# A SwiGLU channel mixer: twelve column pairs as seven half-size products, with the weight sums made by adding DMA transfers

## The chip, the cores and the metric

The kernel runs on one core of one Trainium2 chip. The metric is the device time of one execution in microseconds (us). The core has five engines with a queue each: TensorE (PE; its weight loads are listed apart as PEld), VectorE (DVE), ScalarE (ACT), GpSimd (POOL) and SyncE (SP, which only starts DMA transfers). Sixteen DMA engines move the data; transfers started by SP and ACT go through hardware queues, those started by POOL through a software queue.

## The reference

One encoder block on x of 512 frames by 1024 channels, in float32. Two token mixers (a gated delta rule and a convolution) are merged and added to x; the channel mixer follows:

```python
x = x + (gate_a * out_a + gate_b * out_b) @ w_out[l]

h2 = rmsnorm(x, norm2_w[l])
f_gate, f_up = jnp.split(h2 @ ffn_w_gate_up[l], 2, axis=-1)
x = x + (jax.nn.silu(f_gate) * f_up) @ ffn_w_down[l]
...
return rmsnorm(x, norm_f_w)
```

The hidden width is 2816, that is 22 tiles of 128. `h2 @ ffn_w_gate_up` is the part that the change recasts; `ffn_w_down` is read by both versions in the same seven products.

## The kernel before

Every float32 factor of a large product is split into a high part (type float32r) and a low part. One product of tiles is three matmuls: high by high, high by low, low by high (`split3`, line 107; all matmuls of the large products carry line 113).

**Weights.** `unit` (line 92) brings in 512 KB of weights: SP loads tile `raw` (128x1024), ACT makes the high part `whi` (line 102), DVE the low part `wlo` (line 104). The pool `wp` holds three of each, so a unit's split can begin when PE has finished with the unit three places back.

**Order.** A list scheduler lays out each engine's queue. It takes instructions by priority, which is program order unless an offset is given (`background`, line 618), as soon as operands and buffers are free in its own simulated time. `issue_after` pins one instruction behind another on the same engine. Each engine then executes its queue strictly in order.

**Stages.** The projections of the token mixers run to about 497 us; their last ones are the 16 gate projections, a unit each (line 555), each with a 256 KB store. Then come 8 units of `wo` and 8 of `wpw` (lines 734 to 760), then `tok_mm` with `w_out`, 4 units for each half of the channels (line 763). Its `post`, `norm2`, makes the RMS norm of the rows, whose transposes become `hh` and `hl`, the high and low part of h2 (8 channel tiles of 128x512).

**Gate and up** (line 873). For each of the 22 hidden tiles f two units are used: `wgu[f]` (gate) and `wgu[22 + f]` (up). `col_tile` makes 8 channel tiles x 3 = 24 matmuls of 512 columns for each, so a pair is 48. ACT applies SiLU, DVE multiplies (line 888). The first pair is cut in two halves of 256 columns (`k_loop`). Beside this loop POOL makes the weight sums of the down projection: `sums(k)` (line 860) loads 1 MB of `wdn`, adds four times 128x512 (lines 864 to 867) and writes 1 MB to DRAM. DVE and ACT make the operands of the down projection from the hidden tiles: for f < 11 the split of the first half of the tokens, for f >= 11 sums of two hidden tiles.

**Down** (lines 933 to 1016). Four rounds: `two` runs three times over 11 weight pairs with four 128x512 accumulators (12 matmuls of 512 columns for each weight pair), then the last product, p3. Its six units `ws` are loaded and split (line 994) while `part` consumes them: k = 0 to 5 for both row tiles, k = 6 to 10 for row tile 0, then row tile 1 in two halves of 256 columns. Between the third `two` and p3 the program has `norm_f` of the row tiles (lines 983 to 988): ACT squares (line 794), POOL sums and the power (lines 796, 798), POOL's product of the rows with the norm weight (line 916), ACT's scaling (line 918) and DVE's (line 920), then the stores. The residual y1 stays in SBUF from `tok_mm` to the end.

Of the kernel before, what the change touches and what calls it, by code (L numbers as in the profile page):

```python
# [6 lines left out]
F32 = mybir.dt.float32  # L7
# [23 lines left out]
def block_kernel(ctx, tc, a):  # L31
# [6 lines left out]
    pa_ = ctx.enter_context(tc.tile_pool(name="pA", bufs=1))  # L38
# [53 lines left out]
    def unit(ap):  # L92
        n = 1024
        raw = wp.tile([P, 1024], F32, name="raw")
        if isinstance(ap, tuple):
            n = T * len(ap)
            for i, p in enumerate(ap):
                nc.sync.dma_start(raw[:, i * T:(i + 1) * T], p)
        else:
            nc.sync.dma_start(raw.rearrange("p (a c) -> p a c", a=2) if len(ap.shape) == 3 else raw, ap)  # L100
        hi = wp.tile([P, 1024], F32R, name="whi")
        marked(S.activation(hi[:, 0:n], raw[:, 0:n], AF.Copy), "unit")  # L102
        lo = wp.tile([P, 1024], F32R, name="wlo")
        marked(V.tensor_tensor(out=lo[:, 0:n], in0=raw[:, 0:n], in1=hi[:, 0:n].bitcast(F32), op=ALU.subtract), "unit")  # L104
        return hi, lo
# [28 lines left out]
    cs = []  # L134

# [426 lines left out]
    def ln_mean():  # L562
# [5 lines left out]
        for i in range(KD):  # L568
            V.tensor_tensor(out=cv[i], in0=cv[i], in1=mu, op=ALU.subtract)
            if i == 0:  # L570
                S.activation(vacc, cv[i], AF.Square)
            else:
                sq2 = tp.tile([P, T], F32, name="acc4")
                S.activation(sq2, cv[i], AF.Square)
                G.tensor_tensor(out=vacc, in0=vacc, in1=sq2, op=ALU.add)
# [111 lines left out]
    last = [None]  # L687
# [74 lines left out]

    def tok_mm(wname, kts, xh, xl, post, between):


        for hf in range(2):
# [25 lines left out]
    def rms_half(ss, hf, n, cs, sq, last):  # L792
# [47 lines left out]
    keep.close()  # L840


    fp = ctx.enter_context(tc.tile_pool(name="fp", bufs=2))
    nfw = fp.tile([P, D], F32, name="nfw", bufs=1)
    nc.gpsimd.dma_start(nfw, a["nfw"].partition_broadcast(P))
    FK = FF // 2

    def xset():

        return fp.tile([P, T], F32R, name="fh", bufs=FK + 2), fp.tile([P, T], F32R, name="fl", bufs=FK + 2)  # L850

# [3 lines left out]


# [3 lines left out]
    def sums(k):  # L860
        r = fp.tile([P, 4, T], F32, name="wst", bufs=1)
        nc.gpsimd.dma_start(r, a["wdn"][k].rearrange("p (i c) -> p i c", i=4))
        b11, b12, b21, b22 = (r[:, i, :] for i in range(4))
        G.tensor_tensor(out=b11, in0=b12, in1=b11, op=ALU.subtract)  # L864
        G.tensor_tensor(out=b12, in0=b22, in1=b12, op=ALU.subtract)
        G.tensor_tensor(out=b22, in0=b22, in1=b11, op=ALU.subtract)
        G.tensor_tensor(out=b21, in0=b22, in1=b21, op=ALU.subtract)
        nc.gpsimd.dma_start(wsum[k], r)

    TH = T // 2  # L870
    t1, t2 = slice(0, TH), slice(TH, T)
    fms, set1 = [], []
    for f in range(FF):
# [6 lines left out]
        sg = fp.tile([P, T], F32, name="fsg")  # L880
# [5 lines left out]
        fm = fp.tile([P, T], F32, name="fm", bufs=FF)  # L886
        fms.append(fm)
        V.tensor_tensor(out=fm, in0=pu, in1=sg, op=ALU.mult)  # L888
        if f < FK:
            sums(f)  # L890
            set1.append(xset())
            hi, lo = (t[:, t1] for t in set1[f])
            xsplit(hi, lo, fm[:, t1])
        else:

            b = fms[f - FK]
            s1 = fp.tile([P, TH], F32, name="s1")
            V.tensor_tensor(out=s1, in0=b[:, t2], in1=fm[:, t2], op=ALU.add)
            hi, lo = (t[:, t2] for t in set1[f - FK])
            xsplit(hi, lo, s1)  # L900
            V.tensor_tensor(out=b[:, t2], in0=b[:, t1], in1=b[:, t2], op=ALU.subtract)
            V.tensor_tensor(out=b[:, t1], in0=s1, in1=b[:, t1], op=ALU.subtract)


    hps.close()
    dp = ctx.enter_context(tc.tile_pool(name="dp", bufs=2, side="right"))
    ss3 = dp.tile([P, 5, NT], F32, name="ss3", bufs=1)
    o0 = [dp.tile([P, T], F32, name="o0", bufs=NT) for _ in range(NT)]
    c1, c2 = slice(0, T), slice(T, D)

    def norm_f(hf, n, cs):
        last = hf == 4 or hf == 1 and n != 1
        rms_half(ss3, hf, n, cs, dp.tile([P, T], F32, name="rms_sq", bufs=1)[:, 0:cs.stop - cs.start], last)
        rs = ss3[:, 3, n:n + 1]
        if hf == 0:
            G.tensor_tensor(out=o0[n], in0=y1[:, n, cs], in1=nfw[:, cs], op=ALU.mult)
        if last:
            S.activation(o0[n], o0[n], AF.Copy, scale=rs)
            o1 = dp.tile([P, T], F32, name="o1")
            V.scalar_tensor_tensor(out=o1, in0=y1[:, n, c2], scalar=rs, in1=nfw[:, c2], op0=ALU.mult, op1=ALU.mult)  # L920
# [154 lines left out]
```

## Time and profile before

| | |
|---|---|
| runs shown | 988.28, 990.41, 992.32 us; median 990.41 |
| the profiled execution | 987.57 us, its span 985.8 us |
| mean granted TensorE clock | 0.994 |
| PE busy | 955.7 us of the span (97%) |
| DVE, ACT, POOL busy | 669.8, 513.6, 255.1 us |
| moved by DMA | 138.50 MB, mean 140 GB/s |

A row of a timeline has start, duration, engine, line, operation, output <- inputs, and in brackets how long the engine had been idle and what ended that. A row of groups has the line, engine, operation and shapes, the count, then busy us and the mean ns of one, then the idle time before them. A row of a chain of waits has start, duration, engine, output and line. A row of windows has the stretch, its length, then the busy time (and instruction count) of PE, PEld, DVE, ACT and POOL, the granted clock, the share of the 16 DMA engines, and GB/s. A matmul's duration runs from its start to its modelled end; matmuls overlap, so the pace is read from start to start.

### The profile page before, as it was taken

To read this page: it belongs to the slowest core of one execution; us is meant where nothing else is said; L and a number is where in the kernel's file an instruction comes from. 1 tells how busy PE (TensorE), PEld (TensorE's weight loads), DVE (VectorE), ACT (ScalarE), POOL (GpSimd) and SP (SyncE) were. 2 spreads that over 40 slices of the span, in tenths; PEclk is the share of its full clock that TensorE was granted. 3 is DMA by queue.
4 is the path that set the end of the run, shared out by engine and by line. 5 is a ranking of instruction groups with operands and counts; after the bars stand their busy time and mean duration, and the time that the engine had idled before them with its cause. 6 is when DMAs were issued, how large, how long until landed. Compare 5 with 4: busy or idle time off the path is not lost.

```text
span 985.8 us, 13439 instructions
## 1 busy us (share of the span) xinstructions
PE 955.7 (97%) x4775; PEld 785.7 (80%) x4775; DVE 669.8 (68%) x1044; ACT 513.6 (52%) x1062; POOL 255.1 (26%) x410
## 2 busy tenths in 40 slices
PE   7999999999999999999999999999999999999995
PEld 5688878878787778888878888888888888888784
DVE  4899888888787669889578544542434464469953
ACT  6689777777767664543446323432223322256543
POOL 0314543343243240000050001243534432001412
PEclk9999999999999999999999999999999999999997
DMA  8233421413212122234744432556565565256462
GB/s 317 88 119 120 120 91 41 127 68 98 77 65 88 65 87 69 97 124 144 272 137 137 146 115 65 166 192 246 186 242 206 203 211 184 92 168 196 160 207 86
DMA packets 48291, 138.50 MB, mean 140 GB/s; under 512 B 7472, under 2 KB 9424, under 8 KB 45408
## 3 DMA queue, kind: packets, MB, share of 16 engines
q1 hardware_dynamic: 44016, 112.36, 34.4%
q0 software_dynamic: 3488, 24.17, 6.9%
q10 hardware_dynamic: 720, 1.11, 0.3%
q8 instruction: 37, 0.61, 0.3%
q14 instruction: 30, 0.25, 0.1%
HBM read 119.52 MB, written 18.10 MB: 140 GB/s over the span
## 4 chain that ended last, share of the span: by engine, by line
PE 84%; ACT 5%; DVE 4%; POOL 4%; issue 2%; DMA 1%; SPq 0%; POOLq 0%; ACTq 0%; DVEq 0%
PE mm L113 64%; PE w L113 11%; DVE wlo L104 1%; POOL Un L350 1%; ACT cp L355 1%; ACT Un L349 1%; PE st L477 1%; PE b L415 1%; PE b L421 1%; PE st L483 1%; POOL ytm L376 1%; PE st L489 1%; PE g L346 1%; DMA raw<-in_win_dram 1%; PE st L478 1%
## 5 line engine op out<-in xcount | busy, mean ns | idle before, releaser
L102 ACT ACTIVATE whi<-raw 128x1024 fp32r<-128x1024 f32 x167 | 176.1, 1057 | 327.1 <-PE mm L113 191.9
L113 PE MATMUL mm<-hh,whi 128*128 128x512 f32 x816 | 325.9, 400 | 0.0
L113 PE MATMUL mm<-hl,whi 128*128 128x512 f32 x816 | 321.9, 395 | 2.3 <-POOL hl L229 1.6
L113 PE MATMUL mm<-hh,wlo 128*128 128x512 f32 x816 | 322.3, 395 | 0.0
L104 DVE TENSOR_TENSOR wlo<-raw,whi 128x1024 fp32r<-128x1024 f32 x167 | 214.5, 1285 | 114.7 <-ACT whi L102 114.1
L545 DVE SCALAR_TENSOR_TENSOR cps<-c,c31w,cps 128x512 f32<-128x512 f32 x240 | 180.0, 750 | 4.9 <-ACT cps L543 1.0
L113 PEld LDWEIGHTS mm<-hl,whi 128*128 128x128 f32 x816 | 153.5, 188 | 33.0 <-POOL hl L229 2.9
L113 PEld LDWEIGHTS mm<-hh,wlo 128*128 128x128 f32 x816 | 153.4, 188 | 30.1
L113 PEld LDWEIGHTS mm<-hh,whi 128*128 128x128 f32 x816 | 153.5, 188 | 29.2 <-ACT hh L228 0.2
L888 DVE TENSOR_TENSOR fm<-mm,fsg 128x512 f32<-128x512 f32 x21 | 14.5, 692 | 67.0 <-PE mm L113 67.0
L300 DVE SCALAR_TENSOR_TENSOR acc<-mm,c4w,acc 128x509 f32<-128x509 f32 (+2 forms) x72 | 52.6, 738 | 1.5 <-ACT acc L297 1.2
L376 POOL TENSOR_TENSOR ytm<-U,y 128x60 f32<-128x60 f32 (+14 forms) x120 | 36.9, 307 | 60.6 <-DMA U<-sc 51.9
L113 PE MATMUL mm<-yh,whi 128*128 128x512 f32 x128 | 50.6, 396 | 0.0
L113 PE MATMUL mm<-yh,wlo 128*128 128x512 f32 x128 | 49.8, 389 | 0.0
L113 PE MATMUL mm<-yl,whi 128*128 128x512 f32 x128 | 49.8, 389 | 0.0
L113 PE MATMUL w<-whi,fh 128*128 128x512 f32 (+1 forms) x115 | 45.3, 395 | 2.8 <-ACT whi L102 2.8
L113 PE MATMUL w<-wlo,fh 128*128 128x512 f32 (+1 forms) x115 | 45.6, 397 | 2.4 <-DVE wlo L104 2.4
L113 PE MATMUL w<-whi,fl 128*128 128x512 f32 (+1 forms) x115 | 45.0, 393 | 0.0
L378 POOL TENSOR_TENSOR y<-y,ytm 128x60 f32<-128x60 f32 (+14 forms) x120 | 34.9, 291 | 9.4
L511 POOL TENSOR_TENSOR ss<-ss,half 128x4 f32<-128x4 f32 x8 | 8.1, 1014 | 109.5 <-DVE ss L509 109.5
L796 POOL TENSOR_SCALAR ss<-ss 128x1 f32<-128x1 f32 x17 | 5.7, 338 | 117.9 <-ACT sg L794 105.3
L864 POOL TENSOR_TENSOR wst<-wst 128x512 f32<-128x512 f32 x11 | 15.2, 1386 | 62.7 <-DMA wst<-in_wdn_dram 62.7
(288 smaller groups left out, 1489.1 us busy)
## 6 DMA issues: line engine op xcount, KB each, us to landing
raw<-in_win_dram SPq DMA_DIRECT2D x61, 512.0 KB, 3.3
raw<-in_wgu_dram SPq DMA_DIRECT2D x44, 512.0 KB, 3.4
wst<-in_wdn_dram POOLq DMA_DIRECT2D x11, 1024.0 KB, 5.7
wsum<-wst POOLq DMA_DIRECT2D x11, 1024.0 KB, 4.7
raw<-wsum SPq DMA_DIRECT2D x44, 256.0 KB, 3.2
raw<-in_wdn_dram SPq DMA_DIRECT2D x33, 256.0 KB, 2.9
A<-in_x_dram SPq DMA_DIRECT2D x8, 512.0 KB, 6.3
U<-sc SPq DMA_DIRECT2D x64, 64.0 KB, 2.3
```

Of the source, the lines that this page charges most:

```text
L102: marked(S.activation(hi[:, 0:n], raw[:, 0:n], AF.Copy), "unit")
L104: marked(V.tensor_tensor(out=lo[:, 0:n], in0=raw[:, 0:n], in1=hi[:, 0:n].bitcast(F32), op=ALU.subtract), "unit")
L113: marked(PE.matmul(ps, l, r, start=first and i == 0, stop=last and i == 2))
L300: marked(V.scalar_tensor_tensor(out=acc[:, s:], in0=ps[:, :T - s], scalar=c4w[:, j, k:k + 1], in1=acc[:, s:], op0=ALU.mult, op1=ALU.add))
L346: PE.matmul(ps[:, n, :], kT[:, n, :], kT[:, n, :], start=True, stop=True)
L349: S.activation(Un[:, n, :], ps[:, n, :], AF.Copy, scale=nb2[:, n:n + 1])
L350: G.tensor_tensor(out=Un, in0=Un, in1=DT, op=ALU.mult)
L376: G.tensor_tensor(out=tm[:, :, 0:w], in0=U[:, k, :, k + 1:], in1=y[:, :, k:k + 1].broadcast_to([P, NT, w]), op=ALU.mult)
L378: last[0] = G.tensor_tensor(out=y[:, :, k + 1:], in0=y[:, :, k + 1:], in1=tm[:, :, 0:w], op=ALU.add)
L545: V.scalar_tensor_tensor(out=acc, in0=c[:, k:k + T], scalar=c31w[:, i, k:k + 1], in1=acc, op0=ALU.mult, op1=ALU.add)
L864: G.tensor_tensor(out=b11, in0=b12, in1=b11, op=ALU.subtract)
L888: V.tensor_tensor(out=fm, in0=pu, in1=sg, op=ALU.mult)
```

## The change

For f = 0 to 9 gate and up stay as they were. For f = 10 to 21 the pair is treated as a 2x2 block matrix (gate and up, by two halves of the channels) times another (two halves of the channels by two halves of the tokens), and made by seven products (Strassen's scheme in Winograd's form) in place of eight: each is 4 channel tiles x 3 = 12 matmuls of 256 columns, 84 for a pair. The operand sums of h2 (`xb`, T1 to T4) are made once on DVE, POOL and ACT. The four sums of weights for each pair (s1 to s4, 256 KB each) are made in DRAM: SP copies one block, then a POOL transfer adds the other to it. These 48 pairs of transfers are issued one with each `unit`, from step 335 of the first stage on. A pair now takes four units (3.5 x 512 KB).

The weight sums of the down projection (`dsums`, as `sums` before) are spread over f = 1 to 16; five of the eleven lie beside the pairs 10, 11, 13, 14 and 16. The splits of hidden tiles 0 to 9 are made beside the pairs 10 to 14, two for each. Of the sums of hidden tiles two go to POOL. The residual is written to DRAM in `norm2` (`ysp`) and loaded again in the first `two` (`y2`). In `two` the next operands are made two steps later. The norm of the row tiles is spread over the first steps of p3; row tiles 2 and 3 are scaled by DVE in both halves.

```diff
-    def unit(ap):
...
+        for i, p in enumerate(aps):
+            loads.append(nc.sync.dma_start(raw[:, i * T:(i + 1) * T] if len(aps) > 1 else raw, p))
+        if start_feed[0] and feed:
+            feed_one()
...
+    FK, F0 = FF // 2, 10
+    feed = [("s1", 0)] + [w for p in range(FF - F0) for w in (("s3", p), ("s2", p), ("s1", p + 1), ("s4", p))]
+    feed = [(*w, *{"s1": ("A21", gu["A22"]), "s3": ("A11", gu["A21"]), "s2": ("A11", sums["s1"]),
+                   "s4": ("A12", sums["s2"])}[w[0]]) for w in feed if w[1] < FF - F0]
+    def feed_one(n=1):
+        for _ in range(n):
+            if feed:
+                w, p, m, other = feed.pop(0)
+                with tc.issue_after(loads[-1].ins):
+                    nc.sync.dma_start(sums[w][p], gu[m][p])
+                begun.append((sums[w][p], other[p]))
+        while len(begun) > (2 if feed else 0):
+            with tc.issue_after((fed[-1] if fed else last[0]).ins):
+                fed.append(nc.gpsimd.dma_start(*begun.pop(0), accum_op=ALU.add, max_dma_last_dim=2048))
...
+        start_feed[0] = count[0] >= 335
...
+            start_feed[0] = not hf
...
+            nc.scalar.dma_start(ysp[n], y1[:, n, :])
...
+    def operands(f):
+        if f < FK:
+            set1[f] = xset()
+            hi, lo = (t[:, t1] for t in set1[f])
+            xsplit(hi, lo, fms[f][:, t1])
+            return
+        b, fm = fms[f - FK], fms[f]
+        s1 = fq.tile([P, TH], F32, name="s1")
+        tt(s1, b[:, t2], fm[:, t2], ALU.subtract)
+        hi, lo = (t[:, t2] for t in set1[f - FK])
+        xsplit(hi, lo, s1)
+        tt(b[:, t2], b[:, t1], b[:, t2], ALU.subtract, G)
+        tt(b[:, t1], b[:, t2], fm[:, t2], ALU.add, G)
...
+    def dsums_to(f):
+        while nk[0] < FK and f > 3 * nk[0] // 2:
+            dsums(nk[0])
+            nk[0] += 1
...
+    for i, (ks, ts, eng) in enumerate(((kl, t1, V), (kl, t2, V), (kh, t2, V), (kh, t1, G))):
+        xb.append(fx.tile([P, KH, TH], F32, name="xb%d" % i))
+        tt(xb[i], hh[:, ks, ts].bitcast(F32), hl[:, ks, ts].bitcast(F32), ALU.add, eng)
+    b11, b12, b22, b21 = xb
+    tt(b11, b11, b12, ALU.subtract)
+    last[0] = tt(b12, b22, b12, ALU.subtract, G)
+    tt(b22, b22, b11, ALU.add)
+    tt(b21, b22, b21, ALU.subtract)
+    xsplit(*T4, b21)
+    S.activation(T2[0], b22, AF.Copy, scale=-1.0)
+    V.scalar_tensor_tensor(out=T2[1], in0=b22, scalar=-1.0, in1=T2[0].bitcast(F32), op0=ALU.mult, op1=ALU.subtract)
+    xsplit(*T3, b12)
...
+    def hprod(ps, w, i, x):
+        for k in range(KH):
+            c = slice(i * T + k * P, i * T + k * P + P)
+            split3(ps, (w[0][:, c], w[1][:, c]), x[0][:, k, :], x[1][:, k, :], k == 0, k == KH - 1)
...
+    def pair(f):
+        z = [bank() for _ in range(4)] if f % 2 == 0 else [bank(), bank2(), bank2(), bank2()]
+        s = lambda n: sums[n][f - F0]
+        w = unit(a["wgu"][f])
+        w46 = unit((a["wgu"][FF + f][:, T:], s("s2")))
+        hprod(z[0][:, t1], w, 0, B11)
+        hprod(z[1][:, t1], w, 1, B21)
+        hprod(z[2][:, t1], w46, 0, T4)
+        w37 = unit((s("s4"), s("s3")))
+        hprod(z[0][:, t2], w46, 1, T2)
+        cw = fq.tile([P, T], F32, name="cw", bufs=2)
+        S.copy(out=cw[:, t1], in_=z[0][:, t1])
+        u = fq.tile([P, TH], F32, name="cu")
+        tt(u, cw[:, t1], z[0][:, t2], ALU.add)
+        hprod(z[1][:, t2], w37, 0, B22)
+        w5 = unit((s("s1"),))
+        hprod(z[3][:, t1], w37, 1, T3)
+        v = fq.tile([P, TH], F32, name="cv2")
+        tt(v, u, z[3][:, t1], ALU.add)
+        if f == F0:
+            xsplit(*T1, b11)
+        hprod(z[2][:, t2], w5, 0, T1)
+        tt(cw[:, t2], u, z[2][:, t2], ALU.add)
+        fm = hidden()
+        tt(fm.rearrange("p (i t) -> p i t", i=2), z[2].rearrange("p (i t) -> p i t", i=2),
+           v.rearrange("p (a t) -> p a t", a=1).broadcast_to([P, 2, TH]), ALU.add)
+        tt(cw, cw, z[1], ALU.add)
+        S.activation(cw, cw, AF.Silu)
+        V.scalar_tensor_tensor(out=fm, in0=fm, scalar=-1.0, in1=cw, op0=ALU.mult, op1=ALU.mult)
+    for f in range(F0, FF):
+        pair(f)
...
+        dsums_to(f)
+        for i in [i for i in range(F0) if i // 2 == f - F0] + [f]:
+            operands(i)
...
+            if also and k > FK - 6:
+                with tc.issue_after(loads[-1].ins):
+                    nc.sync.dma_start(*also.pop(0))
...
-            then(k)
+            if k > 1:
+                then(k - 2)
+    def set_3(k):
+        set3.append(xset())
+        xsplit(*set3[k], fms[FK + k])
+        tt(fms[k][:, t1], fms[FK + k][:, t1], fms[k][:, t1], ALU.subtract, G)
...
-    for n in range(2):
-        add(2 + n, c1, p4[n], op=ALU.subtract)
-        norm_f(0, 2 + n, c1)
-        norm_f(1, 2 + n, c2)
-        add(n, c1, p2[n])
-        norm_f(0, n, c1)
...
+        if k < 2:
+            add(2 + k, c1, p4[k])
+            squares(0, 2 + k, c1)
+            squares(1, 2 + k, c2, True)
+        elif k < 4:
+            add(k - 2, c1, p2[k - 2])
+            for cs, eng in ((c1, nc.scalar), (c2, nc.sync)):
+                scaled_out(k, cs, eng)
+            first_half(k - 2)
```

More of the change, by code (lines that the diff above doesn't have):

```diff
@@ L90, in behind, with unit @@
             yield
-    def unit(ap):
[L93 to L104, printed above, removed]
+    loads, start_feed = [], [False]
+    last = [None]
+    def unit(ap, pool=None):
+        aps = ap if isinstance(ap, tuple) else (ap,)
+        n = T * len(aps) if isinstance(ap, tuple) else 1024
+        raw, hi, lo = ((pool or wp).tile([P, n if pool else 1024], t, name=x)[:, 0:n]
+                       for t, x in ((F32, "raw"), (F32R, "whi"), (F32R, "wlo")))
+        for i, p in enumerate(aps):
+            loads.append(nc.sync.dma_start(raw[:, i * T:(i + 1) * T] if len(aps) > 1 else raw, p))
+        if start_feed[0] and feed:
+            feed_one()
+        marked(S.activation(hi, raw, AF.Copy), "unit")
+        marked(V.tensor_tensor(out=lo, in0=raw, in1=hi.bitcast(F32), op=ALU.subtract), "unit")
         return hi, lo
@@ L885, in block_kernel @@
             k_loop(*first[1], slice(2 * P, T))
[L886 to L902, printed above, removed]
+        tt(hidden(), pu, sg, ALU.mult)
@@ L907, in block_kernel, with squares @@
+    y2 = dp.tile([P, NT, D], F32, name="y2", bufs=1)
     ss3 = dp.tile([P, 5, NT], F32, name="ss3", bufs=1)
-    o0 = [dp.tile([P, T], F32, name="o0", bufs=NT) for _ in range(NT)]
+    o0 = [dp.tile([P, T], F32, name="o0", bufs=2) for _ in range(2)]
     c1, c2 = slice(0, T), slice(T, D)
[L911 to L920, printed above, removed]
-            nc.scalar.dma_start(a["out"][n][:, c1], o0[n])
-            nc.sync.dma_start(a["out"][n][:, c2], o1)
+    def squares(hf, n, cs, last=False):
+        rms_half(ss3, hf, n, cs, dp.tile([P, T], F32, name="rms_sq", bufs=1)[:, 0:cs.stop - cs.start], last, y2)
@@ L1007, in block_kernel @@
     add(0, c2, p3[0])
-    norm_f(1, 0, c2)
+    squares(1, 0, c2, True)
     add(1, c2, p3[1])
@@ L1015, in block_kernel @@
         add(1, cs, ps)
-        norm_f(4 if c else 1, 1, cs)
+        squares(4 if c else 1, 1, cs, c)
+        if not c:
+            out(0)
+    out(1)
 def _layout(i):
```

136 lines of the change are left out of this document (89 added, 47 removed).

## The prediction

> **What bounds the kernel now.** I read the page first, then the chain of waits, then windows by stage.
>
> ```profile
> PE 955.7 (97%) x4775; PEld 785.7 (80%) x4775; DVE 669.8 (68%) x1044; ACT 513.6 (52%) x1062; POOL 255.1 (26%) x410
> PEclk9999999999999999999999999999999999999997
> q1 hardware_dynamic: 44016, 112.36, 34.4%
> q0 software_dynamic: 3488, 24.17, 6.9%
> ```
>
> PE is busy 97% of the span, at the full granted clock in all slices but the last. So a matmul taken away is worth its pace, and the end has a loss of its own. The chain:
>
> ```profile
> 635.92 228.28 PE mm L113 x1007
> ...
> 956.16 1.85 POOL o L916 x2
> ```
>
> Gate and up is one run of PE without a wait: 228.28 us for 1007 matmuls of 512 columns is 0.2267 us each, start to start, and 48 x 0.2267 = 10.88 us for a pair. In p3, near the end, the chain leaves PE for POOL.
>
> **The change, part by part.** *The seven products.* The trace has matmuls of just their form (weights stationary, 256 columns of h2 moving) in the first pair; these are the fourth and the last of 48:
>
> ```profile
> 622.74 0.28 PE L113 MATMUL w<-hh,whi 128*128 128x256 f32 x1
> ...
> 628.00 0.28 PE L113 MATMUL w<-hh,wlo 128*128 128x256 f32 x1
> ```
>
> 44 intervals in 5.26 us are 0.1195 us each, more than half of 0.2267. So a pair costs 84 x 0.1195 = 10.04 us, not 7/8 of 10.88 (9.52). Saved: 12 x (10.88 - 10.04) = **10.1 us**.
>
> *DVE beside the pairs.* A pair now has 3.5 units to split in place of 2, and six sums to read out. DVE's prices, first where POOL is idle (three neighbours, start to start), then in the gate-and-up loop, then in a stretch where POOL adds tiles:
>
> ```profile
> 936.37 0.41 DVE L854 TENSOR_TENSOR fl<-fm,fh 128x256 fp32r<-128x256 f32 x1
> 936.70 1.21 DVE L104 TENSOR_TENSOR wlo<-raw,whi 128x1024 fp32r<-128x1024 f32 x1
> 937.84 0.75 DVE L854 TENSOR_TENSOR fl<-fm,fh 128x256 fp32r<-128x256 f32 x2
> ```
>
> ```profile
> L104 DVE TENSOR_TENSOR wlo<-raw,whi 128x1024 fp32r<-128x1024 f32 x42 | 57.0, 1357 | 60.0 <-ACT whi L102 60.0
> L865 POOL TENSOR_TENSOR wst<-wst 128x512 f32<-128x512 f32 x11 | 19.0, 1730 | 0.9
> L867 POOL TENSOR_TENSOR wst<-wst 128x512 f32<-128x512 f32 x11 | 16.9, 1539 | 0.9
> L866 POOL TENSOR_TENSOR wst<-wst 128x512 f32<-128x512 f32 x11 | 16.1, 1460 | 0.9
> L864 POOL TENSOR_TENSOR wst<-wst 128x512 f32<-128x512 f32 x11 | 15.2, 1386 | 62.7 <-DMA wst<-in_wdn_dram 62.7
> L888 DVE TENSOR_TENSOR fm<-mm,fsg 128x512 f32<-128x512 f32 x20 | 13.8, 692 | 63.7 <-PE mm L113 63.7
> ```
>
> ```profile
> L104 DVE TENSOR_TENSOR wlo<-raw,whi 128x1024 fp32r<-128x1024 f32 x3 | 6.4, 2132 | 0.0
> L854 DVE TENSOR_TENSOR fl<-fm,fh 128x256 fp32r<-128x256 f32 x6 | 4.5, 780 | 0.0
> 922.88 2.67 POOL L925 TENSOR_TENSOR A<-A,u 128x512 f32<-128x512 f32 x2 [26.49 <-DVE u L964]
> 925.50 7.38 POOL L925 TENSOR_TENSOR A<-A,v 128x512 f32<-128x512 f32 x4
> ```
>
> Undisturbed: a wlo 1.14, 256 columns 0.33, 512 columns 0.69 us. A pair has three wlo and a half (4.11), three sums of 256 (0.99), three operations of 512 (2.07) and two for its operands (0.66): 7.83 us; the pairs 10 to 14 make two more splits, 8.49 each, but pair 10 has no sum, so 42.1 us for the five, against 5 x 10.04 = 50.2 us of PE. But four of the spread POOL sums lie beside them, 1.73 + 1.54 + 1.46 + 1.39 = 6.12 us each, and eight POOL operations of 256 columns (an estimate, half of 1.39): 24.5 + 5.5 = 30.0 us of POOL. In the disturbed stretch, 924.8 to 935.2 us, DVE's work of 3 x 1.14 + 6 x 0.33 = 5.4 us took 10.4, 5.0 lost to 8.1 us of POOL (all of the last row, and 0.7 of the one before): 0.62 us lost per POOL us when DVE always has work. In the loop before, where DVE waits more than it works, 42 wlo lost 42 x (1.357 - 1.21) = 6.2 to 67.2 us of POOL, 0.09. So the five pairs need 42.1 + 2.7 = 44.8 to 42.1 + 18.6 = 60.7 us: PE waits 0 to 10.3 us. DVE would be at some 85%, between the two rows; with 0.4 it needs 54.1. I take **4 us** lost. The pairs 15 to 21 have one POOL sum and 70.3 us of PE for 7 x 7.83 = 54.8 of DVE: nothing.
>
> The Trainium skill ("SBUF — State Buffer", section "Who interferes with whom") says that a DVE instruction with two SBUF inputs contends with a GpSimd instruction that reads SBUF, and that the shared ports are held for the whole of an instruction while the other is fully blocked. Half agrees: exclusive, the disturbed stretch would have taken 5.4 + 8.1 = 13.5 us, not 10.4. What it would make of the five pairs is the first rival below.
>
> *The tail.* Here is p3 on PE, and the other engines beside it:
>
> ```profile
> 963.43 0.39 PE L113 MATMUL mm<-wlo,fh 128*128 128x512 f32 x1
> 966.66 0.50 PE L113 MATMUL w<-whi,fh 128*128 128x512 f32 x1 [2.84 <-ACT whi L102]
> ...
> 968.74 0.79 PE L113 MATMUL w<-wlo,fh 128*128 128x512 f32 x1 [1.35 <-DVE wlo L104]
> 969.33 0.63 PE L113 MATMUL w<-whi,fh 128*128 128x512 f32 x1
> 969.75 0.63 PE L113 MATMUL w<-whi,fl 128*128 128x512 f32 x1
> ...
> 977.80 0.28 PE L113 MATMUL mm<-wlo,fh 128*128 128x256 f32 x1
> ```
>
> ```profile
> 956.16 4.78 POOL L916 TENSOR_TENSOR o<-A,nfw 128x512 f32<-128x512 f32 x3 [23.28 <-DVE A L925]
> 963.57 0.72 ACT L918 ACTIVATE o<-o,ss 128x512 f32<-128x512 f32 x1 [4.85 <-POOL ss L798]
> 965.56 1.04 ACT L102 ACTIVATE whi<-raw 128x1024 fp32r<-128x1024 f32 x1
> ```
>
> POOL multiplies rows for 4.78 us before it reaches the sums of squares; ACT's scaling stands idle for them 4.85 us, and the fourth unit's whi is queued behind it. PE waits twice, and then its pace is 0.42 us (969.33 to 969.75): the clock was withdrawn. After 963.43 there are 15 matmuls of 512 and 30 of 256 columns left, 15 x 0.2267 + 30 x 0.1195 = 7.0 us, which would have ended at 970.7; they ended at 977.9. Loss 7.2 us. In the change row tiles 2 and 3 need no POOL product, and ACT has nothing that waits for POOL ahead of the last `out`. DVE gets two more scalings beside three wlo, so a microsecond may stay: gain **6.5 us**, between 0 and 7.2. The end behind PE's last matmul keeps its steps.
>
> *The third round.* Two waits when POOL adds p6 and p7:
>
> ```profile
> 930.35 0.50 PE L113 MATMUL w<-wlo,fh 128*128 128x512 f32 x1 [0.42 <-DVE wlo L104]
> ...
> 934.02 0.50 PE L113 MATMUL w<-wlo,fh 128*128 128x512 f32 x1 [0.65 <-DVE wlo L104]
> ```
>
> Together 1.1 us. In these steps DVE loses one subtraction to POOL, which makes it in the round before: gain 0 to 1.1, taken **0.6**.
>
> *The feed.* 48 copies on SP behind a unit's load, and 48 adding transfers on POOL. No transfer that adds is in the trace. The DMA engines' pace: 34.4% of 985.8 us for 112.36 MB is 331 GB/s, 6.9% for 24.17 MB is 355 GB/s; so a copy of 256 KB takes 0.79 us of all sixteen, an adding one at least a pass (0.74), at most three (two reads, a write, 2.2). I take two, 1.5, the middle. The tightest stretch is the gate projections:
>
> ```profile
> 442.00:497.00 55.00, 55.00 (x249) 45.53 (x247) 40.19 (x51) 21.71 (x32) 1.12 (x2) 1.00 0.59 200
> 497.00:575.00 78.00, 78.00 (x342) 63.73 (x341) 58.27 (x67) 37.64 (x49) 12.40 (x7) 1.00 0.43 137
> ```
>
> A unit lasts 24 x 0.2267 = 5.44 us, with 0.59 x 5.44 = 3.2 us of DMA; 3.2 + 0.79 + 1.5 = 5.5. Ten units lose 0 to 7.5 us (three passes); with loads up to two units ahead I take **1 us** lost. Later the share is 0.43, room enough.
>
> *The rest.* Four residual stores are issued by ACT in `norm2`; an issue takes it 0.36 us:
>
> ```profile
> 978.70 0.36 ACTq L921 DMA_DIRECT2D out_dram<-o  x1
> ```
>
> The last stands before the splits that the first pair needs: 0.4 us lost. The residual's loads ask in four steps of 12 x 0.2267 = 2.72 us for 1.58 us of DMA beside 1.58: 0.44 x 4 = 1.8 us late, covered by the units loaded ahead; nothing. The operand sums of h2 (some ten DVE operations, 12 us) need only hh and hl, and DVE was idle 60.0 us before wlo alone in that loop (L104's row above): nothing. If they were queued only behind f = 9, PE would wait for T4 after 24 matmuls: seven DVE operations, 8 us, and ACT's split, 1, less 2.9, about 6 us.
>
> *Sum*: -10.1 - 6.5 - 0.6 + 4 + 1 + 0.4 = -11.8 us. The profiled execution took 987.57 us (span 985.8), so 975.8; the median of the runs, 990.41, lies 2.84 above it, so **978.6 us**.
>
> **The rivals.** *DVE and POOL shut each other out* in the pairs 10 to 14: 42.1 + 16 x 1.39 + 5.5 = 69.8 us against 50.2, 19.6 lost in place of 4: 994.2. For it: 2132 ns for a wlo; against it: the overlap in that very stretch. The Trainium skill's "SBUF — State Buffer" has it as the rule quoted above.
>
> *The tail keeps its wait*, because ACT or DVE is queued badly again: 978.6 + 6.5 = 985.1. For it: DVE's added scalings; against it: the multiplications that stood in front are gone.
>
> *Slower: the adding transfers fill the DMA engines.* Place: the 38 units from the gates to `w_out`. If POOL's queue always has work, SP's gets half of the engines: a load (1.58), a copy and a store or gate load (0.79 each), 3.16, take 6.32 us, 0.88 more than a unit's 5.44. 38 x 0.88 = 33 less two units' head start (10.9): 22.5 us, so 978.6 - 1 + 22.5 = 1000.1. It decides from 5.44 - 3.16 = 2.3 us for an adding transfer, just above three passes. For it: no such transfer is known here; against it: the share of 0.43 from 497 us.
>
> *All of it works*: no wait in the pairs, the feed or the tail: 990.41 - 10.1 - 7.2 - 1.1 + 0.4 = 972.4.
>
> **How the numbers follow.** Forecast 50% (its own range 971 to 986), DVE and POOL 14%, tail 14%, slower 12%, all works 10%. Half a percent, 5 us, is about what a measurement of this kernel can tell from no change: 985.5 and 995.4 are the bounds. Faster: 47 + 10 + 8 (half of the tail's and more) + 2 = 67%; same: 3 + 6 + 11 = 20%; slower 12 + 1 = 13%. The range 968 to 995 takes in the bounds of DVE's loss and of the tail and leaves out the full DMA.
>
> **What would show it.** Right: the new 256-column matmuls 0.12 us apart; the twelve pairs in about 125 us; PE's waits there on wlo, in the pairs beside POOL's sums; no wait over 1 us in p3 and a last slice of the clock at 9; the DMA share of the gates near 0.9 without waits of PE. Wrong: PE waiting for whi or raw between 442 and 690 us, wlo means near 2 us through all of the pairs, a gap of PE at the first pair before T4, or a pace above 0.13 us.

## The result, and the profile after

The changed kernel takes **993.82 us** (median of 20 runs, 990.53 to 999.15) against 988.73 us for the kernel before (20 runs beside it, 987.37 to 992.32). The ratio is 1.0054, with a 95% interval of 1.004 to 1.0068: **slower by some 5 us**, where 11.8 us less than before, 978.6 us, was forecast. The profiled execution has a span of 995.7 us, 9.9 more than before's 985.8; it is one of the slower ones (997.49 us, 3.7 above its median), so some of what the two traces differ by is the spread of executions.

The page of the changed kernel first: the engines, the clock by slice, the DMA queue of POOL (packets, MB, share of sixteen engines), and from the list of DMA issues the copies and the loads of the finished weight sums (count, KB each, median us from issue to landing):

```profile
PE 953.4 (96%) x5207; PEld 802.0 (81%) x5207; DVE 735.7 (74%) x1107; ACT 537.6 (54%) x1100; POOL 336.9 (34%) x491
PEclk9999999999999999999999999999999999999999
q0 software_dynamic: 10400, 36.75, 14.8%
s<-in_wgu_dram SPq DMA_DIRECT2D x48, 256.0 KB, 5.9
raw<-s SPq DMA_DIRECT2D x48, 256.0 KB, 4.2
```

PE's busy time fell by 2.3 us only, not by the 10.1 forecast for the pairs. DVE got 66 us more work, POOL 82. The last slice of the clock is now a 9. To find the place, I cut both traces at the same matmuls: the first of pair 10, the first of `down`, the last. One fence for each kernel, before and then after, from PE's timeline:

```profile
864.04 0.39 PE L113 MATMUL w<-whi,fh 128*128 128x512 f32 x1
```

```profile
743.64 0.28 PE L117 MATMUL w<-hh,whi 128*128 128x256 f32 x1
...
879.44 0.40 PE L117 MATMUL w<-whi,fh 128*128 128x512 f32 x1
...
987.95 0.28 PE L117 MATMUL mm<-wlo,fh 128*128 128x256 f32 x1
```

The kernel before makes its pairs at 10.88 us each without a wait, so its pair 10 began at 864.04 - 12 x 10.88 = 733.5. That gives

| stretch | before | after | forecast of the difference | measured |
|---|---|---|---|---|
| start to pair 10 | 733.5 | 743.6 | +1.4 (feed, residual stores) | **+10.1** |
| pairs 10 to 21 | 130.6 | 135.8 | -6.1 (-10.1 + 4) | **+5.2** |
| `down` to the last matmul | 113.8 | 108.5 | -7.1 | -5.3 |

The first term is seven times its forecast, the second has the other sign; the third came nearly as forecast.

**Ahead of the pairs.** The chain of waits there (start, us, what ran or ended the wait):

```profile
631.46 9.81 DMA s<-in_wgu_dram
...
642.58 2.43 POOL xb L894
645.01 1.24 POOL wst L894
646.25 2.35 POOL xb L894
648.86 2.00 issue
...
651.46 1.71 DVE xb L894
653.16 2.22 DVE wlo L108
655.43 88.38 PE mm L117 x382
```

PE waits for a `wlo`, which DVE makes late; DVE is late because its next operand sum (`xb`) needs one of POOL; and POOL made that only when a copy of 9.81 us had landed. The same in PE's timeline, in POOL's, and in the view of waits (us in total, times, longest; the first row for the whole span, the second from 620 to 880 us), all of the changed kernel:

```profile
650.68 0.50 PE L117 MATMUL mm<-hh,whi 128*128 128x512 f32 x1 [0.76 <-ACT whi L107]
655.43 0.80 PE L117 MATMUL mm<-hh,wlo 128*128 128x512 f32 x1 [4.01 <-DVE wlo L108]
```

```profile
634.01 0.85 POOL L165 DMA_DIRECT2D s<-in_wgu_dram  x1 [1.34 <-DMA s<-in_wgu_dram]
...
641.77 0.81 POOL L165 DMA_DIRECT2D s<-s  x1 [6.90 <-DMA s<-in_wgu_dram]
642.32 2.69 POOL L894 TENSOR_TENSOR xb<-hh,hl 128x1024 f32<-128x1024 f32 x1
```

```profile
POOL s L165 <- DMA s<-in_wgu_dram: 159.8, 36, 9.1
...
DVE xb L894 <- POOL xb L894: 9.9, 1, 9.9
```

The kernel before has neither of these two waits. An adding transfer cannot be issued before its copy has landed, and while it stands at the head of POOL's queue nothing behind it runs: 159.8 us in all, 6.90 of them just ahead of the sum that DVE needs. Between the same two matmuls, at 637.8 and 660.5 us of the kernel before, the changed kernel falls 6.8 us further behind. That is more than the 4.8 us of PE's two waits, because the clock fell behind them (granted clock, the column after POOL; from 655.3 to 658.6 us it was 0.50):

```profile
638.00:660.00 22.00, 17.23 (x74) 13.69 (x73) 12.14 (x10) 6.50 (x8) 13.84 (x9) 0.92 0.50 148
660.00:743.60 83.60, 83.60 (x370) 69.25 (x369) 31.12 (x25) 20.85 (x24) 36.81 (x33) 1.00 0.73 247
```

**In the pairs.** At PE's pace they need 12 x 10.04 = 120.5 us; they took 135.8. The two parts of the stretch, DVE's groups in it, then the timelines of POOL, DVE and PE at the worst place:

```profile
743.60:794.00 50.40, 47.36 (x379) 46.92 (x379) 40.04 (x57) 23.22 (x38) 18.03 (x15) 0.97 0.75 264
794.00:879.40 85.40, 79.68 (x632) 77.57 (x631) 71.32 (x93) 37.69 (x55) 41.33 (x37) 0.98 0.70 232
```

```profile
L108 DVE TENSOR_TENSOR wlo<-raw,whi 128x1024 fp32r<-128x1024 f32 x36 | 49.0, 1362 | 16.3 <-ACT whi L107 15.6 <-PE w L117 0.5
L891 DVE TENSOR_TENSOR fl<-fm,fh 128x256 fp32r<-128x256 f32 x11 | 8.0, 763 | 0.5 <-ACT fh L890 0.5
```

```profile
758.31 6.35 POOL L894 TENSOR_TENSOR wst<-wst 128x512 f32<-128x512 f32 x4 [6.87 <-DMA wst<-in_wdn_dram]
```

```profile
760.56 5.05 DVE L891 TENSOR_TENSOR fl<-fm,fh 128x256 fp32r<-128x256 f32 x5
765.54 1.21 DVE L108 TENSOR_TENSOR wlo<-raw,whi 128x1024 fp32r<-128x1024 f32 x1
```

```profile
766.80 0.38 PE L117 MATMUL w<-hh,wlo 128*128 128x256 f32 x1 [2.61 <-DVE wlo L108]
...
768.27 0.42 PE L117 MATMUL w<-hh,whi 128*128 128x256 f32 x1
768.48 0.41 PE L117 MATMUL w<-hl,whi 128*128 128x256 f32 x1
```

Five splits of 256 columns took 1.01 us each in the mean in place of 0.33, while POOL was adding weight sums; the `wlo` behind them came late, PE waited 2.61 us and then ran at 0.21 in place of 0.12 us. PE's waits in the pairs are 8.7 us of the 15.3 lost; the rest is pace, 3.4 us of it in two stretches, from 767.9 and from 802.0 us, of 3.4 us each at a granted clock of 0.50. But DVE is busy only 79% and 84% of the two parts, and the view of waits has it idle for ACT's `whi` again and again; ACT, in turn, waits for the weights' landing (waits from 743.6 to 879.4 us):

```profile
ACT whi L107 <- DMA raw<-s: 21.8, 19, 3.3
```

That points to a second thing at work: a load that is issued late.

### The profile page after: what moved, and what is told of

The parts are those of the page before. It is cut to its first block, busy times and chain, and to the rows that moved or that the text cites. A ratio compares the mean times of both kernels' runs of the same rounds, so it can differ in the third digit from the quotient of the medians.

```text
span 995.7 us, 14753 instructions
## 1 busy us (share of the span) xinstructions
PE 953.4 (96%) x5207; PEld 802.0 (81%) x5207; DVE 735.7 (74%) x1107; ACT 537.6 (54%) x1100; POOL 336.9 (34%) x491
## 3 DMA queue, kind: packets, MB, share of 16 engines
q0 software_dynamic: 10400, 36.75, 14.8%
## 4 chain that ended last, share of the span: by engine, by line
PE 70%; DVE 9%; DMA 6%; ACT 6%; POOL 5%; issue 3%; SPq 0%; ACTq 0%; POOLq 0%; DVEq 0%
PE mm L117 48%; PE w L117 13%; DVE wlo L108 5%; DMA raw<-s 3%; ACT whi L107 2%; DMA s<-in_wgu_dram 2%; POOL sacc L606 1%; POOL Un L381 1%; DVE cw L894 1%; ACT cp L386 1%; ACT Un L380 1%; PE st L508 1%; PE b L446 1%; PE b L452 1%; PE st L514 1%
## 5 line engine op out<-in xcount | busy, mean ns | idle before, releaser
L107 ACT ACTIVATE whi<-raw 128x1024 fp32r<-128x1024 f32 (+1 forms) x191 | 195.9, 1028 | 264.5 <-PE mm L117 180.2
L108 DVE TENSOR_TENSOR wlo<-raw,whi 128x1024 fp32r<-128x1024 f32 (+1 forms) x191 | 247.1, 1295 | 99.8 <-ACT whi L107 97.7
L117 PE MATMUL mm<-hh,wlo 128*128 128x512 f32 (+1 forms) x696 | 269.6, 387 | 4.1 <-DVE wlo L108 4.0
L117 PE MATMUL mm<-hh,whi 128*128 128x512 f32 (+1 forms) x696 | 272.7, 392 | 0.8 <-ACT whi L107 0.8
L117 PE MATMUL mm<-hl,whi 128*128 128x512 f32 (+1 forms) x696 | 268.9, 386 | 2.3 <-POOL hl L260 1.6
L894 POOL TENSOR_TENSOR wst<-wst 128x512 f32<-128x512 f32 x44 | 70.0, 1592 | 51.2 <-DMA wst<-in_wdn_dram 49.0
L117 PE MATMUL w<-hh,wlo 128*128 128x256 f32 x152 | 45.1, 297 | 5.3 <-DVE wlo L108 5.3
L894 POOL TENSOR_TENSOR fm<-fm 128x256 f32<-128x256 f32 x33 | 33.3, 1019 | 38.4 <-DVE fl L891 19.2
L117 PE MATMUL w<-hh,whi 128*128 128x256 f32 x152 | 44.0, 291 | 1.6 <-ACT whi L107 1.4
L117 PE MATMUL w<-hl,whi 128*128 128x256 f32 x152 | 44.0, 290 | 1.0 <-DVE hl L864 1.0
```

The source lines that it names most:

```text
L107: marked(S.activation(hi, raw, AF.Copy), "unit")
L108: marked(V.tensor_tensor(out=lo, in0=raw, in1=hi.bitcast(F32), op=ALU.subtract), "unit")
L117: marked(PE.matmul(ps, l, r, start=first and i == 0, stop=last and i == 2))
L894: return eng.tensor_tensor(out=out, in0=in0, in1=in1, op=op)
```

## Experiments

Four theories. **Q**: POOL's queue, standing on adding transfers, delays the operand sum; this is what is lost ahead of the pairs. **C**: in the pairs, POOL's sums and DVE slow each other, as the forecast's term has it, only more. **R**: in the pairs, the three `raw` buffers are too few: a unit lasts 1.44 to 2.88 us of PE where it was 5.44, a late `wlo` frees its buffer late, the next load is issued late and lands 4.2 us later, and the next `wlo` is late. **F**: the feed's traffic on the DMA engines is what costs.

The kernels of 1 to 5 and of 8 were timed once each. The pairs of four kernels that do the same work there (`xb_dve`, the changed kernel, `lag6`, `no_feed`) took 134.8, 135.8, 136.9 and 137.6 us, so a difference of 3 us between two profiles says little (the pairs of 6 and 9 differ by 4.4).

**1. Both of POOL's operand sums on DVE** (`xb_dve`).

```diff
-    for i, (ks, ts, eng) in enumerate(((kl, t1, V), (kl, t2, V), (kh, t2, V), (kh, t1, G))):
+    for i, (ks, ts, eng) in enumerate(((kl, t1, V), (kl, t2, V), (kh, t2, V), (kh, t1, V))):
...
-    last[0] = tt(b12, b22, b12, ALU.subtract, G)
+    tt(b12, b22, b12, ALU.subtract)
```

> The changed kernel with the two operand sums of h2 that POOL makes (the fourth xb and b12) made by DVE instead. Theory Q (POOL's queue stands behind adding transfers that wait for their copies, and DVE's queue stands behind POOL's sum): the wait of PE of 4.2 us before the matmul at 655.43 and the 0.9 us before it go, the twelve pairs begin 5 to 6 us earlier than 743.6 us. Theory F (the DMA engines are full and the weight loads late): nothing changes, or 1 us more for DVE's two longer sums. Both: the twelve pairs stay at 134 to 138 us.

Measured: 988.84 us. Its chain, then its first matmuls of the pairs and of `down`:

```profile
638.32 97.72 PE mm L117 x431
```

```profile
735.88 0.28 PE L117 MATMUL w<-hh,whi 128*128 128x256 f32 x1
...
870.69 0.40 PE L117 MATMUL w<-whi,fh 128*128 128x512 f32 x1
```

From 638.32 us on 431 matmuls without a wait: the pairs begin at 735.88, 7.8 us earlier, though POOL still waits 150.9 us for copies. Of the 7.8 us, 6.8 lie between the two matmuls named above (637.8 and 660.5 us of the kernel before), where `xb_dve` loses nothing. It does not hang on one trace: the kernels below that leave these two sums on POOL and keep the feed lose 3.5 to 6.7 us there (`quiet_pairs` 3.7, `raw4` 6.7, `raw4_quiet` 3.5, `lag6` 4.1), and those with the sums on DVE lose nothing. The pairs take 134.8 us, hardly less. Q holds for the first stretch, and says nothing of the second.

**2. No copies and no adding transfers** (`no_feed`); the products' loads read blocks of `wgu` of the same size, so the output is not the block's, and the loads of `wdn` no longer stand behind the last adding transfer.

```diff
-                    nc.sync.dma_start(sums[w][p], gu[m][p])
...
-                fed.append(nc.gpsimd.dma_start(*begun.pop(0), accum_op=ALU.add, max_dma_last_dim=2048))
...
-        s = lambda n: sums[n][f - F0]
+        s = lambda n: gu[{"s1": "A21", "s2": "A11", "s3": "A11", "s4": "A12"}[n]][f - F0]
```

> The changed kernel without the 48 copies and the 48 adding transfers; the loads of the sums read blocks of the gate-and-up weights in their place, as large as before, so the output of the pairs 10 to 21 is not the block's. Theory Q and theory F alike: the 1.1 us at the convolution's norm (518 us) and the 6.6 us between 632 and 656 us go, the pairs begin near 735 us; DMA share of the gates back from 0.94 to about 0.6. It tells what the feed costs in all. The feed is over before the pairs, so they stay at 134 to 138 us if POOL's sums or the loads' round trip make them slow, and fall below 130 only if the feed still disturbs them.

Measured: 990.45 us. The pairs begin at 735.44 us, the same gain as in `xb_dve` within 0.5 us, and take 137.6 us, no less than with the feed. So the transfers cost nothing in the pairs: F falls there. Ahead of the pairs this run cannot tell Q from F; `xb_dve` can, since it keeps every transfer and loses nothing between 638 us and the pairs.

**3. The spread sums from the seventh on not added** (`quiet_pairs`): the loads and stores stay, POOL's four additions are gone.

```diff
-        tt(b22, b12, b22, ALU.add, G)
-        tt(b12, b11, b12, ALU.add, G)
-        tt(b11, b22, b11, ALU.add, G)
-        tt(b21, b11, b21, ALU.add, G)
+        if k < 6:
+            tt(b22, b12, b22, ALU.add, G)
+            ...
```

> The changed kernel without the four POOL additions of the last five weight sums of the down projection (k = 6 to 10), those beside the pairs; their loads and stores stay, so the output is not the block's. Theory C (POOL's additions slow DVE, the low parts come late): the twelve pairs fall from 135.8 to 123 to 128 us, and the wait of 2.8 us in pair 12 with the slow clock behind it goes. Theory R (a raw buffer is loaded again only when its low part is made, and the load's round trip is too long for three short units): the pairs stay at 132 us or more.

Measured: 984.72 us; the pairs run from 739.25 to 866.80, 127.6 us. DVE's groups in them:

```profile
L108 DVE TENSOR_TENSOR wlo<-raw,whi 128x1024 fp32r<-128x1024 f32 x36 | 45.1, 1253 | 22.2 <-ACT whi L107 21.7 <-PE mm L117 0.5
L891 DVE TENSOR_TENSOR fl<-fm,fh 128x256 fp32r<-128x256 f32 x11 | 4.7, 465 | 0.5 <-ACT fh L890 0.5
```

8.2 of the 15.3 us go with POOL's additions; the splits of 256 columns fall from 763 to 465 ns, the long ones from 1362 to 1253. The granted clock is 1.00 through these pairs, so the 3.4 us of the two slow stretches are among the 8.2. C holds for some half.

**4. Four `raw` buffers in place of three** (`raw4`); the additions stay.

```diff
-        raw, hi, lo = ((pool or wp).tile([P, n if pool else 1024], t, name=x)[:, 0:n]
+        raw, hi, lo = (wp.tile([P, 1024], t, name=x, bufs=4 if x == "raw" else 3)[:, 0:n]
```

> The changed kernel with four raw buffers in place of three (high and low parts stay at three). Theory R: a load can start a unit earlier, the pairs fall from 135.8 to 123 to 128 us, and raw is gone from PE's chain there. Theory C: the pairs stay at 132 us or more. Before the pairs nothing changes by more than 1 us.

Measured: 984.84 us; the pairs run from 741.21 to 867.93, 126.7 us: 9.1 of the 15.3 go, with POOL at its additions as before. In the part from 744 to 858 us ACT's waits for landings fall from 19.7 us (16 times) in the changed kernel to

```profile
ACT whi L107 <- DMA raw<-s: 8.0, 8, 1.8
```

R holds for some half too. That nothing would change by more than 1 us before the pairs failed: between 235 and 372 us, in the token mixers, this kernel wins 2.2 us on the changed one, and so do the other four with a fourth buffer (2.2 to 2.3).

**5. Both** (`raw4_quiet`: the diffs of 3 and 4 together).

> The changed kernel with four raw buffers and without the POOL additions of the last five weight sums (the output is not the block's). If both edits took away one and the same wait, a low part that comes late and its load's round trip behind it, the pairs reach nearly the pace of PE, 121 to 123 us. If they took away different waits, each about 8 us, the pairs end at 121 us as well but then each alone must have left a wait of the other's kind. If another wait remains that neither touches, 125 us or more.

Measured: 974.91 us. The pairs run from 737.69 to 858.97, 121.3 us, PE's own pace within 1 us, and the chain through their start has no wait:

```profile
737.85 11.51 PE w L117 x96
749.37 2.88 PE mm L117 x24
```

PE has no wait at all in these pairs. 8.2 and 9.1 make 17.3, and there were 15.3 to get; together the edits get 14.5. So the two gains add up, but for an overlap of 2.8 us that is no larger than what two profiles differ by. Each edit alone left waits of the other's kind: ACT still waits 15.1 us (11 times) for landings in `quiet_pairs`, and in `raw4` PE's waits are for a `wlo` (4.1 of 4.3 us). I read C and R as meeting in one loop (POOL's additions make a `wlo` late, and the buffer that it frees late makes the next one late); that they do is not shown by these times, only that the two together make up nearly all of the loss. PE's wait of 3.1 us ahead of the pairs is still there, as Q has it, since this kernel leaves POOL's `xb` where it was.

**6. The two mended together** (`raw4_xb`: the diffs of 1 and 4, all sums made).

> The changed kernel with four raw buffers and both operand sums on DVE. If the waits before the pairs and in the pairs are separate, the gains add up: the pairs begin near 736 us and take 125 to 128 us, the time is 13 to 16 us under the changed kernel's 993.8, that is 978 to 981, 1% under the kernel before. If the 7 us won before the pairs only lets the pairs meet the weight sums of the down projection at another point, the pairs take 132 us or more and the time is 985 or more.

Measured: 978.62 us, ratio 0.9891 (0.985 to 0.9931); the pairs run from 731.72 to 860.50, 128.8 us. That this is the time forecast for the change is chance: 8.3 us are still lost in the pairs, and 2.2 us are won in the token mixers, where nothing was forecast. The expectation for this run too came out in its sum only: the pairs began 4 us earlier than its 736 us, and took 0.8 us longer than its 128.

**7. The tail alone on the kernel before** (`tail_only`): its row sums in the order that the change gives them, nothing else.

```diff
-    for n in range(2):
-        add(2 + n, c1, p4[n], op=ALU.subtract)
-        norm_f(0, 2 + n, c1)
-        norm_f(1, 2 + n, c2)
-        add(n, c1, p2[n])
-        norm_f(0, n, c1)
...
+        if k < 2:
+            add(2 + k, c1, p4[k], op=ALU.subtract)
+            squares(0, 2 + k, c1)
+            squares(1, 2 + k, c2, True)
+        elif k < 4:
+            add(k - 2, c1, p2[k - 2])
+            ...
```

> The kernel before with one part of the change alone: the norm of the row tiles spread over the first steps of p3, row tiles 2 and 3 scaled by DVE (the additions keep the signs of before). The tail's theory of the prediction: the two waits of PE at 963 to 969 us (3.0 and 1.5 us above the pace) and the slow clock behind them go, 6.5 us faster (5 to 7.2), all else equal. Rival: the wait only moves (DVE's added scalings hold back the last low parts), less than 2 us faster.

Measured: 982.55 us, ratio 0.9926 (0.9898 to 0.9955). PE's timeline, from the first matmul of `down` to the last:

```profile
866.40 0.39 PE L113 MATMUL w<-whi,fh 128*128 128x512 f32 x1
...
972.84 0.28 PE L113 MATMUL mm<-wlo,fh 128*128 128x256 f32 x1
```

106.4 us against 113.8, 7.4 less: the whole 7.2 us that the forecast had found there, and by itself a faster kernel than the whole change.

**8. The adding transfers further behind their copies** (`lag6`): the program writes an add six copies later in place of two.

```diff
-        while len(begun) > (2 if feed else 0):
+        while len(begun) > (6 if feed else 0):
```

> The changed kernel with six copies begun ahead of an adding transfer in place of two. Theory Q: POOL's queue no longer waits for copies (159.8 us of waits in the changed kernel, under 60 here), and the wait at the convolution's norm (1.1 us, POOL's sums of squares behind an adding transfer) goes. The adding transfers pile up later, so the wait of PE at 651 us may stay. Theory F (the engines are full): POOL's waits stay above 120 us, since the copies themselves land late.

Measured: 995.73 us, and POOL's entry hardly moves:

```profile
POOL s L165 <- DMA s<-in_wgu_dram: 153.5, 35, 9.0
```

This expectation of Q failed, and by its words (waits above 120 us) the outcome is F's. But the edit did not move the adding transfers: the first is issued at 370.5 us (371.3 in the changed kernel), one beside the convolution's norm at 510.1 (510.2). The order in the program is not the order in POOL's queue, which the scheduler lays out. So the run decides nothing between Q and F. That POOL's queue holds the sum up stays shown (by 1); that a larger lag in the program would free it is refuted.

**9. The operand sums behind the last split of h2** (`raw4_xb_hl`, on top of 6). In the changed kernel PE waits 0.99 us for an `hl` at 633 us, behind an `xb` on DVE.

```diff
-            V.tensor_tensor(out=hl[:, k4, ts], in0=ps, in1=hh[:, k4, ts].bitcast(F32), op=ALU.subtract)
+            hl_last[0] = V.tensor_tensor(out=hl[:, k4, ts], in0=ps, in1=hh[:, k4, ts].bitcast(F32), op=ALU.subtract)
...
-        tt(xb[i], hh[:, ks, ts].bitcast(F32), hl[:, ks, ts].bitcast(F32), ALU.add, eng)
+        with tc.issue_after(hl_last[0].ins):
+            tt(xb[i], hh[:, ks, ts].bitcast(F32), hl[:, ks, ts].bitcast(F32), ALU.add, eng)
```

> The changed kernel with four raw buffers, both operand sums on DVE, and the operand sums of h2 issued behind the last low part of h2. The 1.15 us wait of PE before the second matmul of the first pair's second half (a sum of h2 stands on DVE before a low part of h2) goes: 1 us under raw4_xb, 977 to 979; if that wait has another cause it stays, and the time with it.

Measured: 978.23 us, ratio 0.9897 (0.9861 to 0.9933). The wait is gone from the trace, and with it 1.0 us between 624 and 638 us; the time cannot be told from 6. The profiled execution is the slowest of the six (985.43 us). Its pairs take 133.2 us (735.31 to 868.49) where those of 6, the same code, took 128.8; two stretches of 3.4 us at half the granted clock, which 6 does not have, are 3.4 us more. So a fourth buffer with all additions made gives pairs of 126.7 to 133.2 us, against 134.8 to 137.6 with three.

**10. And the last five spread sums later** (`raw4_xb_hl_late`, on top of 9), at pairs 15 to 19, where DVE has no second split.

```diff
-        while nk[0] < FK and f > 3 * nk[0] // 2:
+        while nk[0] < FK and f > (3 * nk[0] // 2 if nk[0] < 6 else nk[0] + 8):
```

> As raw4_xb_hl, with the last five weight sums of the down projection beside the pairs 15 to 19 in place of 10, 11, 13, 14 and 16, so that the pairs in which DVE makes two splits more have no POOL additions beside them. Theory C: DVE has 8.5 us of work in the pairs 10 to 14 and 7.8 in the others, so the waits of PE in the twelve pairs fall from 7.4 us to 2 to 5 us, the time to 973 to 977. If only the amount of POOL's work beside the pairs counts, and not its place, the pairs stay at 127 to 129 us.

Measured: **977.21 us, ratio 0.9882 (0.9865 to 0.9898)**, the lowest but for `raw4_quiet`, which leaves additions out, though it cannot be told from 6 and 9; 1.2% below the kernel before. But PE's waits in the pairs are 5.9 us (5.2 in 6), not the 2 to 5 expected, and the pairs take 130.6 us (731.77 to 862.34), 1.7 of them by a stretch at half the clock. So moving the additions won nothing that shows, and the expectation failed; whether their amount alone counts is not shown either. How the 10 us that are left divide between C and R was not taken apart further; a fifth buffer was not tried.

## Why the prediction was wrong

**The pace, right.** 0.12 us for a 256-column matmul; `raw4_quiet` made the twelve pairs in 121.3 us for 120.5 forecast.

**The tail, right.** 6.5 forecast between 0 and 7.2; 7.4 in `tail_only`. In the changed kernel PE has no wait in p3. `down` as a whole won only 5.3, since the third round (from 941.2 us) kept its two waits and the second got one:

```profile
917.06 0.50 PE L117 MATMUL w<-wlo,fh 128*128 128x512 f32 x1 [1.29 <-DVE wlo L108]
...
947.80 0.50 PE L117 MATMUL w<-wlo,fh 128*128 128x512 f32 x1 [0.53 <-DVE wlo L108]
951.48 0.50 PE L117 MATMUL w<-wlo,fh 128*128 128x512 f32 x1 [0.65 <-DVE wlo L108]
```

So the step that gave 0.6 us for the third round was wrong: the two waits, 0.42 and 0.65 us before, are still there.

**"The operand sums of h2 ... nothing": the step that failed first.** It asked whether DVE had time for them, and it had. Two of the sums are POOL's, and what stood in POOL's queue was not asked. The 6 us priced there were for another mishap (sums queued behind f = 9); the sums were issued early, and POOL reached them late. Cost: 6.8 us between 638 and 660 us, for nothing forecast; 3.5 to 6.7 in the other kernels that leave these sums on POOL behind the feed. And on DVE itself a sum stood in front of a split of h2: 1.0 us more, at 633 us (experiment 9).

**"The feed ... 1 us": right for the DMA engines, blind for the queue.** The gates' share of the DMA engines was forecast at 0.9 without waits of PE for weights, and is 0.94:

```profile
442.00:497.00 55.00, 55.00 (x248) 45.51 (x247) 41.38 (x53) 21.77 (x33) 9.01 (x11) 1.00 0.94 287
```

An adding transfer takes 1.65 us of the sixteen engines (14.8% of 995.7 less 6.9% of 985.8 is 79.3 us, for 48), close to the 1.5 taken. But the time that POOL stands at its queue's head for a copy was no term of the sum. It also holds up the sums of squares behind the convolution, and PE with them (its timeline):

```profile
516.87 1.12 PE L611 MATMUL mm<-sacc,cst 128*128 128x512 f32 x2 [0.89 <-POOL sacc L606]
```

**"DVE beside the pairs ... 4 us", with 10.3 as its upper bound: 15.3.** Four parts of the step failed. First, each pair was summed as work against time, as if a unit could be fetched whenever DVE was ready; the round trip of a `raw` buffer, harmless at 5.44 us a unit, was left out (R, up to 9.1 us). Second, "the pairs 15 to 21 have one POOL sum": they have 35.1 us of POOL (from 800.9 to 879.4 us). POOL's queue again:

```profile
811.82 6.59 POOL L894 TENSOR_TENSOR wst<-wst 128x512 f32<-128x512 f32 x4 [5.15 <-DMA wst<-in_wdn_dram]
818.71 0.55 POOL L933 DMA_DIRECT2D wsum<-wst  x1 [0.30 <-POOL wst L894]
825.17 0.55 POOL L927 DMA_DIRECT2D wst<-in_wdn_dram  x1 [5.91 <-DMA wsum<-wst]
831.56 3.18 POOL L894 TENSOR_TENSOR wst<-wst 128x512 f32<-128x512 f32 x2 [5.84 <-DMA wst<-in_wdn_dram]
...
842.47 12.64 POOL L894 TENSOR_TENSOR fm<-fm 128x256 f32<-128x256 f32 x12
```

One `wst` buffer, loaded, added and stored in turn, takes 18 to 19 us a sum, so the sums trail into the pairs after 15, and the eight operations on `fm` that I had put beside the pairs 10 to 14 came at 834 us or later, most of them in the row at 842. By pairs, 7.1 us were lost in 10 to 14 (57.3 for 50.2) and 8.2 in 15 to 21 (78.5 for 70.3), where the step had nothing. Third, PE's pace after a wait: half pace for some microseconds had been seen in p3 and was not priced here; it is 3.4 us of the 15.3. It is not a sure cost: in `xb_dve` the granted clock was 1.00 through the pairs, which took 134.8 us all the same. Fourth, the price itself. The 8.1 us of POOL in the disturbed stretch, which gave 0.62 us lost for each, hold POOL's own waits for DVE: an addition of 128x512 takes POOL 1.29 us beside an idle DVE (at 638.66 us of the kernel before, for one), and 1.30 to 2.28 there. Four of them and 0.7 us of a fifth are 5.9 us, and 5.9 + 5.4 = 11.3 one after the other, close to the 10.4 measured. So the 13.5 us, by which the prediction took the two to exclude each other by half only, came of a misreading. And the step's upper bound is 60.7 - 50.2 = 10.5 by its own figures, not 10.3.

**The rivals.** DVE and POOL shutting each other out was put at 994.2 us, and the time came within 0.4 of it; that is luck. It put 19.6 us into the pairs 10 to 14, where 7.1 were lost, and nothing ahead of them. With POOL's additions gone 7.1 us stayed (`quiet_pairs`), which that rival cannot explain, and nearly all went when a fourth buffer was added. The tail did not keep its wait. The DMA engines were not full: PE waited for no weights in the gates, and `no_feed` gained in front of the pairs only, as `xb_dve` did. The loss of the feed was one of order, where the rival had it as one of bandwidth.

**The sum after the fact**, in the profile: +10.16 ahead of the pairs, +5.24 in them, -5.25 in `down`, -0.22 behind the last matmul: 9.9 us. Of the 10.16, 1.2 are there at 245 us already, before the first copy is issued at 330, so they are not the feed's: from 180 to 190 us the granted clock was 0.83 where it was 1.00 before, which is 1.7 us. Another 1.1 are lost at the convolution's norm (517 us), 1.2 around 633 us, and 6.8 between 638 and 660. Kernels with the same code up to the pairs (`raw4`, but for its buffer, `quiet_pairs`, `raw4_quiet`) begin them at 737.7 to 741.2, so others of these executions lose 4 to 8 us there, which would go some way to explain that the medians differ by 5.1 us where the two profiles differ by 9.9.

## What to carry to other kernels

For each instruction that a change adds to an in-order queue, ask what it waits for and what stands behind it: a transfer that waits for another transfer is a stall for everything on the engine that issues it, however little the engine is busy. Where a change makes the units of a pipeline shorter, work out the round trip of their buffers anew (landing, split, last use, next issue), not only the work of each engine against the time of the stretch. And take a change with separable parts apart first: here the reordered tail alone was worth 0.74%, and the rest of the change hid it.

## What was not expected of the hardware

DVE's short operations suffer most, in proportion, from POOL's additions: over the pairs the duration of a split of 256 columns goes from 0.41 to 0.76 us in the mean, where that of a `wlo` of 1024 goes from 1.21 to 1.36. At the worst place it is as if each DVE operation waited for the end of a POOL one. POOL's additions end at 761.78, 763.24 and 764.65 us, and three of the five splits end 0.3 us behind one each; the two behind them, beside no addition, follow 0.33 us apart. One of each, from the timelines of DVE and POOL:

```profile
762.00 1.52 DVE L891 TENSOR_TENSOR fl<-fm,fh 128x256 fp32r<-128x256 f32 x1
```

```profile
761.87 1.37 POOL L894 TENSOR_TENSOR wst<-wst 128x512 f32<-128x512 f32 x1
```

The rule of the Trainium skill ("SBUF — State Buffer", section "Who interferes with whom"), that the shared ports are held exclusively, fits this row, and, with POOL's own waits taken out, the disturbed stretch in the prediction (11.3 us against 10.4) as well.

The granted clock fell to 0.50 for one stretch of 3.4 us, a loss of 1.7, beside waits of PE of 1.05 us (at 182 us of the changed kernel) to 4.01 us, and not beside others as long (3.11 us in `raw4_quiet`, 2.8 in `xb_dve`: 1.00). In 6 and 9, whose pairs have the same code, such stretches are 3.4 of the 4.4 us by which the pairs differ.

An adding transfer of 256 KB between two places in DRAM took 1.65 us of the sixteen DMA engines, about twice the estimate of 0.79 for a plain copy; POOL is 0.81 us in the median at issuing one (0.80 to 1.16), 0.55 to 0.61 for a plain load or store of weight sums. A copy lands 5.9 us after its issue in the median, and it is this latency, not the 1.65 us, that POOL waited for. Why it is so long was not taken apart.
